# Thirty-two bytes more between the buffers of three tile pools in a one-core decoder trunk

## The chip, the core and the metric

The kernel runs on one core of one Trainium2 chip. The metric is the time of one execution in microseconds (us), the median of a few runs. TensorE multiplies, VectorE (DVE in the profile) and ScalarE (ACT) do the elementwise work, GpSimd (POOL) a little of it, and SyncE (SP) issues the loads of the weights. A matrix product is two instructions: a load of the stationary operand (LDWEIGHTS, the row PEld of the profile) and the streaming of the moving operand (MATMUL, the row PE). Both operands come from the on-chip memory SBUF, which has 128 partitions. A tile lies at the same byte address in every partition. In this document the **place** of a tile is its byte address in the partition modulo 128.

## The reference

Two decoder layers on 256 tokens of width 1024, all in float32. Cut to what matters:

```python
def swiglu_ffn(x, w_in, w_out):                # w_in 1024 x 5632, w_out 2816 x 1024
    gate, up = jnp.split(x @ w_in, 2, axis=-1)
    return (jax.nn.silu(gate) * up) @ w_out

for i in range(2):
    if i == 1:
        kv = shared_kv(h, ...)                 # K and V of three branches, once
    h = h + 0.5 * swiglu_ffn(rmsnorm(h, ffn1_norm[i]), ffn1_w_in[i], ffn1_w_out[i])
    hn = rmsnorm(h, mix_norm[i])
    if i == 0:
        h = h + short_conv_mixer(hn, ...)      # gated 3-tap convolution, two projections
    else:
        h = h + nsa_mixer(hn, ..., kv)         # sparse attention, 16 heads of 64
    h = h + 0.5 * swiglu_ffn(rmsnorm(h, ffn2_norm[i]), ffn2_w_in[i], ffn2_w_out[i])
```

## The kernel before

Tokens stand in the free dimension. Each number is split in two parts, a rounded high part and the rest, both of type float32r. A product of two numbers is then high x high, low x high and high x low. `ScalarE` casts the high part and `VectorE` subtracts to get the low part, for the weights as they arrive (`Stream.high` L250 and `Stream.low` L278, into the tiles `wh` and `wl`) and for the activations.

The normed activations are eight tiles of the pool `xs` (`new_xs`, L395), one for each 128 of the 1024 channels, with 512 columns: 256 tokens high and 256 tokens low. `a_pass` (through `half`, L487) takes a 128x128 piece of `wh` as the stationary operand and streams all 512 columns of one `xs` tile past it, then a piece of `wl` with the 256 high columns alone. So a projection is a long row of alternating groups: matmuls of 512 columns with `wh`, matmuls of 256 columns with `wl`. `xs` tiles are also the stationary operand in the query projection (`q_step`, L1398 to L1400), and hold copied probabilities in attention.

The second projections of three of the feed-forwards go through a blocked product that saves multiplications (`Blocks.product`, L821). There the activations are stationary and the weights stream, always 512 columns. Its stationary tiles are mostly `act`; the sums that it needs of activations lie in the pools `pr` and `hm` (`first_home` L793, `sum_home` L1665), and a few of its streamed weight sums in `pr`, `t2` and `xs` (`second_home`, L318). In attention `pr` holds the scores and probabilities of a head (`minima` L1480, `exps` L1492), and `hm` the values `V` (L1099).

The order of all work is written out by hand or follows from the code; tiles take the next free buffer of their pool. A pool gives each tag as many buffers as asked for, side by side, each as large as the largest tile of that tag. SBUF is filled in this order: constants, among them `ones` at byte 640 (place 0) and `base` at byte 1152; a 32-byte tile; then `ws`, `xs` (from byte 53792), `sq`, `kt`, `wh`, `wl`, `t2`, `t1`, `R`, `act`, `pr`, `sm`, `hm`, `u`, `rc`. All of the large buffers from `ws` to `hm` measure a multiple of 128 bytes (`xs` 2048, `wh` 4096, `act` 2048, `pr` 3072, `hm` 2048), and 24 `sm` buffers of 64 bytes make up 1536. So every large buffer has place 32. Pieces inside them begin at multiples of 512 bytes, so nearly every matmul of type float32r has both operands at place 32. Tiles that differ: `ones` has place 0, the identity in `small` place 0, the residual stream and the staged weights inside `base` place 80, and `vc` place 64.

Of the kernel before, what the change touches and what calls it, by code (L numbers as in the profile page):

```python
# [10 lines left out]
F32R = mybir.dt.float32r  # L11
# [5 lines left out]
P = 128  # L17
# [45 lines left out]
def trunk(ctx, tc, A, out):  # L63
# [11 lines left out]
    def mk(shape, tag, bufs, dt=F32, pool=None):  # L75
        uid[0] += 1
        return (pool or sb).tile(list(shape), dt, tag=tag, name=f"{tag}_{uid[0]}", bufs=bufs)
# [10 lines left out]
    def act(shape=(P, 512), dt=F32R):  # L88
        return mk(shape, "act", 22, dt)
# [4 lines left out]
    def t1(shape=(P, T)):  # L94
        return mk(shape, "t1", 6)

    def sm(shape):
        return mk(shape, "sm", 24)
# [294 lines left out]


    def new_xs():  # L395
        return [mk([P, 512], "xs", 8, F32R) for _ in range(8)]

    class Norm:

# [299 lines left out]


    xs = new_xs()
    nm = Norm([(xs, G_FFN1)])

# [92 lines left out]
    X = {}  # L796
# [161 lines left out]
    def conv_norm():  # L958
        X["xs"] = new_xs()
        X["nm"] = Norm([(X["xs"], G_MIX)])  # L960
        return X["nm"]
# [29 lines left out]
    xs, nm = X["xs"], X["nm"]  # L991
    for f in range(1, 8):
# [18 lines left out]
        weave(todo, 1 if f == 7 else 3)  # L1011

    xs = new_xs()
    nm = Norm([(xs, G_FFN2)])
    tab = tables()
# [80 lines left out]


    KC = (16, 272)
    V = [mk([P, 512], "hm", 5) for _ in range(2)]  # L1099

    vc = one([P, 2, 2, 64], "vc", F32R)
    zero = t2()
# [49 lines left out]
    xs = new_xs()  # L1152
# [3 lines left out]
    for tt in range(2):  # L1156
        ac.activation(V[tt], ov[tt], AF.Copy, scale=rc[:, tt:tt + 1])
    W.limit = 5
# [161 lines left out]
    xs = new_xs()  # L1320
# [158 lines left out]

    def minima(j, g2):  # L1480
        s, t = X.pop(("s", j, g2)), bias[j][:, g2, ::-1]
        X["pr", j, g2], X["mx", j, g2] = pr, mx = mk([P, 768], "pr", 6), sm([P, 16])
        for n, (a, b) in enumerate(SC):
            c0, w = REG[n]
            ve.tensor_tensor_reduce(out=pr[:, c0:c0 + w], in0=t[:, 128:256] if n < 2 else t, in1=s[:, a:b], op0=ALU.add, op1=ALU.min,  # L1485
                                    scale=1.0, scalar=3e38, accum_out=mx[:, n:n + 1])
        if ("cb", j // 2) not in X:
            X["cb", j // 2] = t1([P, 2, 2, 2, 16])
        ve.tensor_tensor(out=X["cb", j // 2][:, j % 2, :, g2], in0=cbias[:, j, :, g2],
                         in1=s[:, :576].rearrange("p (a b) -> p a b", a=2)[:, :, :16], op=ALU.add)  # L1490
# [40 lines left out]
    def copied(key, t, eng):  # L1531
        eng(out=t, in_=X.pop(key))
        X["p", *key[1:]] = t

    def value_codes(j, first=False):
        if first:
            X["v", j] = bank([P, T])
        pe.matmul(X["v", j], vc[:, j // 4].rearrange("p g d -> p (g d)"), ct.pop(j), start=first, stop=not first)

    def values(j, part=""):  # L1540
# [3 lines left out]
        for b in range(2):  # L1544
            for g2 in range(2):
                rows, c0 = slice(g2 * 64, g2 * 64 + 64), b * 256 + (2 * pp + g2) * 64
                pe.matmul(o[rows], V[0][:, c0:c0 + 64], lo[g2][:, b], start=(b == 0 and part != "n"), stop=False)  # L1547
        for b in range(2):
            for g2 in range(2):
                rows, c0 = slice(g2 * 64, g2 * 64 + 64), b * 256 + (2 * pp + g2) * 64  # L1550
                pe.matmul(o[rows, P:], V[1][:, c0:c0 + 64], hi[:, g2, b], start=False, stop=(b == 1 and part == "n"))
        X["v", j] = o
# [59 lines left out]
    def wo_part(c, part):  # L1612
# [10 lines left out]
        "SQ": q_square, "RD": q_reduce, "PW": q_power, "NW": q_newton, "QM": q_normed, "QT": q_trans, "QC": q_gain,  # L1623
        "F": lambda: next(lq), "GT": g_sum, "GC": g_copy, "GA": g_total, "GX": g_trans, "GE": g_exp, "GD": g_out,
        "S": scores, "M": minima, "E": exps, "R": recip,
        "N": lambda j, g, e="": normed(j, g, ve if e else po), "T": trans, "H": trans_hi,
        "C": lambda j, g, e="": copied(("t", j, g), mk([P, 2, T], "xs", 8), copy[e]),
        "CH": lambda j, e="": copied(("t", j), act([P, 2, 2, P], F32), copy[e]),
        "V": values, "VB": lambda j: value_codes(j, True), "O": out_hi, "P": out_lo,
        "CM": c_min, "CX": c_less, "CE": c_exp, "CR": c_recip, "CG": c_gate, "CI": c_high, "CL": c_low, "CP": c_trans,  # L1630
# [10 lines left out]
    xs = new_xs()  # L1641
# [189 lines left out]
```

## Time and profile before

| what | value |
|---|---|
| median of 3 runs | 959.15 us (958.61 to 959.93) |
| the profiled execution, its own time | 959.4 us |
| span of the profiled execution, first to last instruction | 957.5 us |
| granted TensorE clock, mean | 1.000 |
| VectorE busy | 803.5 us (84%) |
| ScalarE busy | 613.0 us (64%) |
| GpSimd busy | 144.5 us (15%) |
| DMA, mean over the span | 187 GB/s |

Busy time is the sum over an engine's instructions, with overlaps counted once. TensorE's matmuls overlap one another, since a matmul's record reaches until its last column has left the array. The mean duration of a matmul row is therefore longer than the distance from one start to the next. What a matmul costs in a long row of matmuls is that distance, called the **pitch** here.

### The profile page before, as it was taken

The numbers are of one execution on the slowest core, as the hardware profiler recorded it, in microseconds if no ns is written. First come the engines' busy times: TensorE is split into PE (matmuls) and PEld (weight loads), VectorE is DVE, ScalarE is ACT, GpSimd is POOL, SyncE is SP. The second block draws the span as 40 slices with busy tenths as digits, with TensorE's granted clock in tenths as the row PEclk, the third lists the DMA queues.
The fourth block names the chain that finished last, engine by engine and source line by source line (L and its number), as shares of the span: only waits on it lengthen the run. The fifth ranks groups of instructions, "written<-read, shape, count | busy, mean of one in ns | idle before, by whom it ended". The sixth has DMA issues, their size and how long they took to land.

```text
span 957.5 us, 14525 instructions
## 1 busy us (share of the span) xinstructions
PE 951.2 (99%) x5431; PEld 827.5 (86%) x5431; DVE 803.5 (84%) x1332; ACT 613.0 (64%) x1048; POOL 144.5 (15%) x231
## 2 busy tenths in 40 slices
PE   8999999999999999999999999999999999999998
PEld 7888888888888888888888898889987888888887
DVE  6898899898898888898969787866588888878996
ACT  7666565565556666565857777754579656656553
POOL 1000000024460000000021042001337350000002
PEclk9999999999999999999999999999999999999999
DMA  8665844364546567553636867554520363467452
GB/s 300 230 216 186 307 149 160 132 208 164 201 138 243 197 208 254 175 196 132 220 132 188 265 212 259 177 201 163 215 89 2 132 221 143 166 222 247 148 179 84
DMA packets 42150, 178.58 MB, mean 187 GB/s; under 512 B 3777, under 2 KB 7505, under 8 KB 27105
## 3 DMA queue, kind: packets, MB, share of 16 engines
q1 hardware_dynamic: 42080, 177.67, 54.1%
q8 instruction: 42, 0.69, 0.3%
q14 instruction: 28, 0.22, 0.1%
HBM read 175.52 MB, written 1.08 MB: 184 GB/s over the span
## 4 chain that ended last, share of the span: by engine, by line
PE 97%; DVE 1%; ACT 1%; DMA 1%; SPq 0%; issue 0%
PE mm L487 55%; PE a L487 13%; PE a L821 12%; PE mm L821 5%; PE a L1124 1%; PE mm L1477 1%; PE a L1547 1%; PE mm L728 1%; PE a L1522 1%; PE a L767 1%; DMA base<-in_first_dram 1%; DVE pr L1485 0%; PE a L1217 0%; PE a L1063 0%; PE a L1065 0%; PE a L1064 0%
## 5 line engine op out<-in xcount | busy, mean ns | idle before, releaser
L487 PE MATMUL mm<-xs,wh 128*128 128x512 f32 x1480 | 349.2, 390 | 0.0
L487 PEld LDWEIGHTS mm<-xs,wh 128*128 128x128 f32 x1480 | 273.6, 188 | 54.8 <-DVE xs L410 0.5
L278 DVE TENSOR_TENSOR wl<-ws,wh 128x1024 fp32r<-128x1024 f32 x217 | 271.1, 1258 | 28.2 <-ACT wh L250 18.4
L250 ACT CAST wh<-ws 128x1024 fp32r<-128x1024 f32 x217 | 224.6, 1045 | 14.9 <-PE a L487 7.3
L487 PEld LDWEIGHTS mm<-xs,wl 128*128 128x128 f32 x1480 | 185.2, 192 | 4.2
L487 PE MATMUL mm<-xs,wl 128*128 128x256 f32 x1480 | 187.3, 283 | 0.0
L506 DVE TENSOR_TENSOR t<-mm,t 128x512 f32<-128x512 f32 x95 | 65.2, 686 | 46.2 <-ACT t L505 45.5
L505 ACT COPY t<-mm 128x512 f32<-128x512 f32 x95 | 55.4, 583 | 52.5 <-PE mm L487 51.8
L821 PE MATMUL a<-wh,act 128*128 128x512 f32 x306 | 81.7, 390 | 0.0
L821 PEld LDWEIGHTS a<-wh,act 128*128 128x128 f32 x306 | 57.3, 188 | 11.8
L530 ACT ACTIVATE t<-t 128x256 f32<-128x256 f32 x88 | 36.8, 418 | 45.9 <-DVE t L517 45.7
L487 PE MATMUL a<-act,wh 128*128 128x512 f32 x256 | 60.0, 390 | 0.0
L487 PEld LDWEIGHTS a<-act,wh 128*128 128x128 f32 x256 | 47.5, 188 | 9.4
L499 ACT CAST act<-t 128x256 fp32r<-128x256 f32 x81 | 33.0, 407 | 29.1 <-DVE t L944 18.5
L406 ACT ACTIVATE xs<-base 128x256 fp32r<-128x256 f32 x32 | 16.1, 508 | 50.1 <-DVE base L637 35.2
L517 DVE TENSOR_TENSOR t<-t,R 128x256 f32<-128x256 f32 (+1 forms) x88 | 45.0, 511 | 2.6
L821 PE MATMUL a<-wl,act 128*128 128x512 f32 x153 | 46.9, 389 | 0.0
L184 DVE TENSOR_TENSOR wl<-base,wh 128x1024 fp32r<-128x1024 f32 x38 | 45.6, 1221 | 0.1
L531 DVE TENSOR_TENSOR t<-t,t 128x256 f32<-128x256 f32 x88 | 37.0, 420 | 4.1 <-ACT t L530 4.1
L500 DVE TENSOR_TENSOR act<-t,act 128x256 fp32r<-128x256 f32 x81 | 35.5, 438 | 4.7 <-ACT act L499 4.7
L173 ACT CAST wh<-base 128x1024 fp32r<-128x1024 f32 x33 | 33.6, 1045 | 4.8 <-DVE base L179 3.0
L821 PEld LDWEIGHTS a<-wl,act 128*128 128x128 f32 x153 | 28.7, 188 | 6.0
(361 smaller groups left out, 1405.5 us busy)
## 6 DMA issues: line engine op xcount, KB each, us to landing
ws<-in_ffn_w_in_dram SPq DMA_DIRECT2D x69, 1024.0 KB, 4.9
base<-in_ffn_w_pairs_dram SPq DMA_DIRECT2D x32, 512.0 KB, 4.8
ws<-in_conv_w_in_dram SPq DMA_DIRECT2D x12, 1024.0 KB, 4.8
ws<-in_ffn_w_pairs_dram SPq DMA_DIRECT2D x22, 512.0 KB, 4.9
ws<-in_ffn_w_out_dram SPq DMA_DIRECT2D x11, 1024.0 KB, 4.8
base<-in_ffn_w_in_dram SPq DMA_DIRECT2D x11, 1024.0 KB, 5.3
kt<-in_ffn_w_pairs_dram SPq DMA_DIRECT2D x12, 512.0 KB, 4.5
ws<-in_w_kv_dram SPq DMA_DIRECT2D x6, 1024.0 KB, 4.9
```

The source lines that it names most:

```text
L173: ac.copy(h, src)
L184: ve.tensor_tensor(out=l, in0=src, in1=h.bitcast(F32), op=ALU.subtract)
L250: ac.copy(h, src)
L278: ve.tensor_tensor(out=l, in0=src, in1=h.bitcast(F32), op=ALU.subtract)
L487: pe.matmul(o if x == 0 else o[:, :T], u[x][:, q * P:(q + 1) * P], rhs if x == 0 else rhs[:, :T], start=start, stop=stop, skip_group_check ...
L500: ve.tensor_tensor(out=dst[:, T:], in0=src, in1=dst[:, :T].bitcast(F32), op=ALU.subtract)
L505: ac.copy(r, o[:, :, T:])
L506: ve.tensor_tensor(out=r, in0=o[:, :, :T], in1=r, op=ALU.add)
L517: ve.tensor_tensor(out=r, in0=r, in1=R[:, None, :].to_broadcast([P, n, T]), op=ALU.mult)
L530: ac.activation(s, r[:, 0], AF.Silu)
L531: ve.tensor_tensor(out=s, in0=s, in1=r[:, 1], op=ALU.mult)
L821: pe.matmul(self.m[n], x, w, start=(c == 0), stop=(c == 3 * self.total[n] - 1), skip_group_check=True)
```

## The change

Three pools ask for buffers that are 8 floats, or 32 bytes, longer; the tiles themselves are cut back to their old size.

```diff
     def new_xs():
-        return [mk([P, 512], "xs", 8, F32R) for _ in range(8)]
+        return [mk([P, 520], "xs", 8, F32R)[:, :512] for _ in range(8)]
...
-    V = [mk([P, 512], "hm", 5) for _ in range(2)]
+    V = [mk([P, 520], "hm", 5)[:, :512] for _ in range(2)]
...
     def minima(j, g2):
         s, t = X.pop(("s", j, g2)), bias[j][:, g2, ::-1]
-        X["pr", j, g2], X["mx", j, g2] = pr, mx = mk([P, 768], "pr", 6), sm([P, 16])
+        X["pr", j, g2], X["mx", j, g2] = pr, mx = mk([P, 776], "pr", 6)[:, :768], sm([P, 16])
```

Since all buffers of a tag are as large as its largest tile, this moves every tile of the three pools, also those that other lines ask for. The places of the buffers, in the built program:

| pool | places before | places after |
|---|---|---|
| `xs`, 8 buffers | all 32 | 32, 64, 96, 0, 32, 64, 96, 0 |
| `pr`, 6 buffers | all 32 | 32, 64, 96, 0, 32, 64 |
| `hm`, 5 buffers | all 32 | 96, 0, 32, 64, 96 |
| `sm`, 24 small buffers | 32 and 96 in turn | 96 and 32 in turn |
| `u`, 2 buffers | 32, 64 | 0, 32 |
| `rc`, 2 buffers | 96 | 64 |
| `ws`, `kt`, `wh`, `wl`, `t2`, `t1`, `R`, `act` | 32 | 32 |

The eight longer `xs` buffers add 256 bytes, so what lies between `xs` and `pr` is moved by 256 bytes and keeps its place. The instructions of all engines, their order and their waits are the same in both programs. Only addresses differ. Of the 4,975 float32r matmuls, 16 had operands at different places before the change. After it there are 2,692: 1,332 with 512 columns and 1,360 with 256.

## The prediction

> **What bounds the kernel now.** I read the page's busy times first, then the chain that ended last, then TensorE's waits.
>
> ```profile
> PE 951.2 (99%) x5431; PEld 827.5 (86%) x5431; DVE 803.5 (84%) x1332; ACT 613.0 (64%) x1048; POOL 144.5 (15%) x231
> PE 97%; DVE 1%; ACT 1%; DMA 1%; SPq 0%; issue 0%
> ```
>
> TensorE is busy for 951.2 of 957.5 us, and the chain is TensorE for 97% of its length. Its waits, all of them:
>
> ```profile
> PE mm L728 <- ACT wh L719: 1.4, 2, 1.1
> PE a L376 <- DVE ones L356: 1.1, 1, 1.1
> PE a L1528 <- DVE xs L1532: 0.3, 1, 0.3
> PE a L1522 <- ACT xs L1532: 0.2, 1, 0.2
> ```
>
> They add up to 3.0 us (us in total, times, longest). So the time is the number of matmuls times the pitch of each, plus little. A change of addresses can act in two ways: through the pitch, or through the durations of the other engines where TensorE waits for them.
>
> The pitch comes from the timeline, from one start to the next. For 512 columns I take a stretch of the blocked product; its first and last rows:
>
> ```profile
> 905.80 0.62 PE L821 MATMUL mm<-wl,pr 128*128 128x512 f32 x2
> ...
> 923.25 0.61 PE L821 MATMUL a<-wh,act 128*128 128x512 f32 x2
> ```
>
> The rows from the first up to the last count 77 matmuls, and 923.25 - 905.80 = 17.45 us, so the pitch is 226.6 ns. For 256 columns a stretch of the convolution layer serves:
>
> ```profile
> 199.75 0.28 PE L487 MATMUL mm<-xs,wl 128*128 128x256 f32 x1
> 199.87 0.40 PE L465 MATMUL a<-t,ones 128*128 128x256 f32 x2
> 200.11 1.12 PE L487 MATMUL mm<-xs,wl 128*128 128x256 f32 x8
> 201.07 1.12 PE L487 MATMUL a<-xs,wl 128*128 128x256 f32 x8
> 202.03 1.32 PE L487 MATMUL mm<-xs,wh 128*128 128x512 f32 x5
> ```
>
> Between 200.11 and 202.03 there are 16 matmuls of 256 columns: 1.92 / 16 = 120.0 ns. The 256 columns more of the long one cost 226.6 - 120.0 = 106.6 ns. A matmul therefore costs its columns and about **13.4 ns more** (120.0 - 106.6), whatever its length. That surplus is what a change of places could touch. All float32r operands here, but for 16 matmuls, lie at place 32, so moving and stationary operand always share a place. After the change 2,692 float32r matmuls have unlike places, 2,676 more than before.
>
> **The change part by part: the matmuls.** The edit of `xs` gives most of these 2,676; the edits of `pr` and `hm` give those of the blocked product with a sum as an operand. Is the surplus a collision of two streams at one place? The trace has a small test of it. The stretch above holds two matmuls of the norm's row sums, `a<-t,ones`: `t` has place 32, the stationary `ones` place 0. The load of the second `ones` is the row
>
> ```profile
> 199.88 0.19 PEld L465 LDWEIGHTS a<-t,ones 128*128 128x128 f32 x1
> ```
>
> and the first of the two matmuls streams `t` from 199.87 on, so the load falls into a stream at another place. The two take 200.11 - 199.87 = 0.24 us, 120 ns each, the same as the 256-column neighbours whose places agree. Without the surplus they would take 2 x 106.6 = 213 ns, which would show as 0.21. So the surplus was paid where the places differ. This is one pair, and its only unlike case is 0 against 32.
>
> The second view asks whether any other traffic in SBUF slows a stream. Two input projections with the same code, half a millisecond apart, are these pieces of the chain:
>
> ```profile
> 289.10 111.85 PE mm L487 x644
> 785.72 111.85 PE mm L487 x644
> 289.10:400.95 111.85, 111.85 (x646) 99.03 (x645) 94.96 (x156) 69.85 (x109) 2.65 (x7) 1.00 0.64 220
> 785.72:897.57 111.85, 111.85 (x646) 99.03 (x645) 94.95 (x159) 69.71 (x109) 0.00 (x0) 1.00 0.52 179
> ```
>
> (The lower rows show the window, its length, busy time and count of PE, PEld, DVE, ACT and POOL, the granted clock, the DMA share and GB/s.) With DMA at 64% or 52%, and GpSimd at 2.65 us or none, the 644 matmuls take the same 111.85 us. Half of them have 512 columns and half 256, and 322 x (226.6 + 120.0) = 111.6 us; the pitch alone fills the section. The stream does not notice what others read or write, so moving their targets should not matter to it.
>
> I take **0** for the matmuls. Both ends are kept: if the surplus goes for all 2,676, the gain is 2,676 x 13.4 ns = 35.9 us; if unlike places cost as much again, the loss is 35.9 us. The nearest row is the `ones` pair, and it says 0.
>
> [...]
>
> **The change part by part: the other engines.** VectorE and ScalarE write or read the moved tiles. Operands at two places are already in the trace: tiles in `base` have place 80, `ws` and `kt` place 32.
>
> ```profile
> L184 DVE TENSOR_TENSOR wl<-base,wh 128x1024 fp32r<-128x1024 f32 x38 | 45.6, 1221 | 0.1
> L184 DVE TENSOR_TENSOR wl<-ws,wh 128x1024 fp32r<-128x1024 f32 x27 | 32.3, 1221 | 0.0
> L173 ACT CAST wh<-base 128x1024 fp32r<-128x1024 f32 x33 | 33.6, 1045 | 4.8 <-DVE base L179 3.0 <-DMA base<-in_ffn_w_pairs_dram 1.8
> L173 ACT CAST wh<-ws 128x1024 fp32r<-128x1024 f32 x22 | 22.5, 1048 | 0.9 <-DVE ws L179 0.9
> ```
>
> On VectorE the mean is 1221 ns from either place beside `wh` at 32; on ScalarE it is 1045 and 1048 ns. The largest difference is 3 in 1045, or 0.3%. What is on the path of these engines' work on moved tiles is small. In attention, the longest such piece of the chain and the row of its group are
>
> ```profile
> 713.47 3.52 ACT pr L1496 x16
> L1496 ACT ACTIVATE pr<-pr,sm 128x256 f32<-128x256 f32 x32 | 16.0, 508 | 0.0
> ```
>
> 0.3% of 3.52 us is 0.01 us. The two waits for `xs` at L1522 and L1528 sum to 0.5 us; if they went the gain is 0.5 us, and if they doubled the loss is 0.5 us. I take 0, nearest to the equal durations, and keep +-0.5 us. The rest of these engines' work on moved tiles stands beside the matmuls: VectorE is busy 94.96 of 111.85 us in the fullest section, so it could grow by 16.89 us there, 17.8% of its own work, before that section's matmuls had to wait on its mean rate. No DMA lands in the three pools, and no instruction or wait is added, removed or moved.
>
> **The sum.** Against the profiled execution: 959.4 + 0 (matmuls) + 0 (other engines, +-0.5) = 959.4 us. That is its span of 957.5 us and 1.9 us around it. The median of the runs shown, 959.15, lies 0.25 us lower; I predict the median after as 959.2 us.
>
> **The rivals.**
>
> Faster: the surplus is a collision of two streams at one place, and unlike places remove it. Then 959.4 - 35.9 = 923.5 us, if the splitting of weights keeps up, and VectorE's 94.96 of 111.85 us leaves the room. For it: nearly all pairs are at one place now, and every pitch has the surplus. Against it: the `ones` pair pays the surplus with unlike places. A part of it, say for one of the three new offsets, gives a third, 947.4 us, which the pair at its one offset does not exclude. Chance 0.11.
>
> Slower: a collision that does not exist now is made. Two streams that start at one place might keep step, and with unlike places the load would meet the moving stream on the same part of the memory somewhere in its course. As much again as the surplus would give 959.4 + 35.9 = 995.3 us; a third, 971.4 us. It decides from 1.9 / 2,676 = 0.7 ns a matmul on, since 0.2% of the time, 1.9 us, is about what a measurement of this kernel can tell from no change. For it: no row shows a stream of the length of the projections at unlike places. Against it: the same `ones` pair, at 120 ns, is not slower than its neighbours. Chance 0.09.
>
> That the change doesn't do what it says is not among them: the built addresses show the four places.
>
> **How the numbers follow.** The forecast has 0.80 for itself: the pair at unlike places, the two equal sections, and equal durations from places 32 and 80 all say that places don't matter, and nothing else changes. Faster has 0.11, slower 0.09. The range must hold 0.8. The forecast's own spread is what runs differ by (958.61 to 959.93), with 0.5 us for the waits and some room for a partial effect of about 1 ns a matmul either way, 2.7 us. I take 956.5 to 962.0 us, which leaves out most of both rivals.
>
> **What would show it right or wrong.** Right: the two sections stay at 111.85 us for 644 matmuls, the pitch at 226.6 and 120.0 ns, and L410, L1485 and L1496 keep their means. Wrong through the pitch: the sections get shorter or longer by the same share. Each has three quarters of its 644 matmuls at unlike places, 483, so a full surplus gained or lost would be 6.5 us, and a third 2.2 us. Wrong through the engines: the pitch stays, and TensorE's waits at L1522 and L1528 change. Were the rivals' effects both present at different offsets, the sections' mean would hide them, and the pitch of each `xs` tile would have to be read alone.

## The result and the profile after

| | median us | runs | lowest to highest |
|---|---|---|---|
| before | 959.12 | 4 | 958.61 to 959.93 |
| after | 963.95 | 4 | 963.75 to 964.11 |

The ratio is 1.0052 (95%: 1.0039 to 1.0064). The change makes the kernel about 4.8 us slower. That lies outside the predicted range, 956.5 to 962.0.

The page after the change, and then TensorE's waits (us in total, times, longest); they answer to the rows at the head of the prediction (the chain's shares are the same as there):

```profile
PE 956.4 (99%) x5431; PEld 824.8 (86%) x5431; DVE 804.9 (84%) x1332; ACT 613.6 (64%) x1048; POOL 144.5 (15%) x231
```

```profile
PE a L376 <- DVE ones L356: 1.0, 1, 1.0
PE mm L728 <- ACT wh L719: 0.6, 2, 0.4
PE a L1528 <- DVE xs L1532: 0.4, 1, 0.4
PE a L1522 <- ACT xs L1532: 0.2, 1, 0.2
```

TensorE's busy time grew by 5.2 us (951.2 to 956.4), the span by 4.6 us (957.5 to 962.1). The waits sum to 2.2 us, 0.8 us less than before. So nobody keeps TensorE waiting: its own matmuls take longer. The long pieces in the chain of waits say in which stages (start, length, count):

```profile
24.55 106.32 PE mm L487 x608
290.31 112.64 PE mm L487 x644
495.46 78.34 PE mm L487 x448
788.92 112.77 PE mm L487 x644
```

Before, the first and third of these were 105.59 and 77.82 us, and the two of 644 matmuls 111.85. Every stage grew, by 0.5 to 0.9 us. The timeline shows which of the two kinds of matmul did it. TensorE in the last of these stages, before and then after (start, length, count):

```profile
789.91 4.00 PE L487 MATMUL mm<-xs,wl 128*128 128x256 f32 x32
793.74 7.44 PE L487 MATMUL mm<-xs,wh 128*128 128x512 f32 x32
801.02 4.00 PE L487 MATMUL mm<-xs,wl 128*128 128x256 f32 x32
```

```profile
793.19 3.93 PE L487 MATMUL mm<-xs,wl 128*128 128x256 f32 x32
796.96 7.60 PE L487 MATMUL mm<-xs,wh 128*128 128x512 f32 x32
804.39 3.93 PE L487 MATMUL mm<-xs,wl 128*128 128x256 f32 x32
```

Take differences of starts. 32 matmuls of 256 columns took 3.83 us and take 3.77: the pitch falls from 119.7 to 117.8 ns. 32 of 512 columns took 7.28 us and take 7.43: it rises from 227.5 to 232.2 ns. **Two effects of opposite sign** share each stage, and its length shows only their difference.

The same on the whole trace, from the start of each matmul to the next, summed over a group and compared with before (the stretches in which TensorE waits are in the sums):

| group | matmuls | mean pitch before, after (ns) | change (us) |
|---|---|---|---|
| 512 columns, `xs` past `wh` (L487) | 1,536 | 228.3, 232.5 | +6.55 |
| 256 columns, `xs` past `wl` (L487) | 1,536 | 119.9, 117.8 | -3.10 |
| blocked product (L821), all its pairs | 735 | | +1.53 |
| everything else | | | -0.4 |
| sum | | | +4.57 |

In the blocked product it is the tiles of the moved pools that lengthen. The view of line L821, before and then after (shortest/median/longest record in ns):

```profile
L821 PE MATMUL mm<-wh,act x67: 389/389/389, 131.7 to 941.2; 128*128 128x512 f32 x67
L821 PE MATMUL mm<-wh,pr x48: 389/389/389, 137.9 to 916.7; 128*128 128x512 f32 x48
L821 PE MATMUL mm<-wh,hm x39: 389/389/389, 163.0 to 940.9; 128*128 128x512 f32 x39
```

```profile
L821 PE MATMUL mm<-wh,act x67: 388/389/398, 132.1 to 945.7; 128*128 128x512 f32 x67
L821 PE MATMUL mm<-wh,pr x48: 389/393/404, 138.3 to 921.0; 128*128 128x512 f32 x48
L821 PE MATMUL mm<-wh,hm x39: 387/394/398, 163.7 to 945.4; 128*128 128x512 f32 x39
```

`act`, which kept its place, keeps its median of 389; `pr` and `hm` go to 393 and 394. Before the change all records of these groups were equal to the nanosecond, and now they scatter. The ends of matmul records are modelled, so the records only point at the tiles; the sums in the table go by starts.

VectorE and ScalarE hardly changed: they are busy for 804.9 and 613.6 us, 1.4 and 0.6 us more than before. The groups of operations on moved tiles and on `wl` after the change:

```profile
L184 DVE TENSOR_TENSOR wl<-base,wh 128x1024 fp32r<-128x1024 f32 x38 | 45.6, 1221 | 0.1
L1496 ACT ACTIVATE pr<-pr,sm 128x256 f32<-128x256 f32 x32 | 16.0, 510 | 0.0
```

The first is the same as before, the second 2 ns longer, 0.4%, or 0.06 us over its 32 runs. The other two groups that the prediction named, L410 and L1485, keep their means of 576 and 417 ns.

### The profile page after: what moved, and what is told of

It is laid out like the page before. It is cut to its first block, busy times and chain, and to the rows that moved or that the text cites. A ratio compares the mean times of both kernels' runs of the same rounds, so it can differ in the third digit from the quotient of the medians.

```text
span 962.1 us, 14525 instructions
## 1 busy us (share of the span) xinstructions
PE 956.4 (99%) x5431; PEld 824.8 (86%) x5431; DVE 804.9 (84%) x1332; ACT 613.6 (64%) x1048; POOL 144.5 (15%) x231
## 4 chain that ended last, share of the span: by engine, by line
PE 97%; DVE 1%; ACT 1%; DMA 1%; SPq 0%; issue 0%
PE mm L487 55%; PE a L487 13%; PE a L821 12%; PE mm L821 6%; PE a L1124 1%; PE mm L1477 1%; PE a L1547 1%; PE a L1522 1%; PE mm L728 1%; PE a L767 1%; DMA base<-in_first_dram 1%; DVE pr L1485 0%; PE a L1217 0%; PE a L1063 0%; PE a L1065 0%; PE a L1064 0%
## 5 line engine op out<-in xcount | busy, mean ns | idle before, releaser
L487 PE MATMUL mm<-xs,wh 128*128 128x512 f32 x1480 | 355.4, 395 | 0.0
L487 PEld LDWEIGHTS mm<-xs,wh 128*128 128x128 f32 x1480 | 273.5, 188 | 60.2 <-DVE xs L442 0.2
L487 PEld LDWEIGHTS mm<-xs,wl 128*128 128x128 f32 x1480 | 182.4, 189 | 4.8
L487 PE MATMUL mm<-xs,wl 128*128 128x256 f32 x1480 | 184.5, 281 | 0.0
L505 ACT COPY t<-mm 128x512 f32<-128x512 f32 x95 | 55.4, 583 | 57.4 <-PE mm L487 56.8
L821 PE MATMUL a<-wh,act 128*128 128x512 f32 x306 | 82.1, 391 | 0.0
L821 PEld LDWEIGHTS a<-wh,act 128*128 128x128 f32 x306 | 57.3, 188 | 12.3
L487 PE MATMUL a<-act,wh 128*128 128x512 f32 x256 | 60.1, 390 | 0.0
L487 PEld LDWEIGHTS a<-act,wh 128*128 128x128 f32 x256 | 47.5, 188 | 9.5
L821 PE MATMUL a<-wl,act 128*128 128x512 f32 x153 | 47.0, 390 | 0.0
L184 DVE TENSOR_TENSOR wl<-base,wh 128x1024 fp32r<-128x1024 f32 x38 | 45.6, 1221 | 0.1
L821 PEld LDWEIGHTS a<-wl,act 128*128 128x128 f32 x153 | 28.7, 188 | 6.1
```

Source lines behind the costliest of these rows:

```text
L184: ve.tensor_tensor(out=l, in0=src, in1=h.bitcast(F32), op=ALU.subtract)
L487: pe.matmul(o if x == 0 else o[:, :T], u[x][:, q * P:(q + 1) * P], rhs if x == 0 else rhs[:, :T], start=start, stop=stop, skip_group_check ...
L505: ac.copy(r, o[:, :, T:])
L821: pe.matmul(self.m[n], x, w, start=(c == 0), stop=(c == 3 * self.total[n] - 1), skip_group_check=True)
```

## The experiments

The theory after the result: what counts is where a matmul's moving operand lies against the stationary one that is being loaded or used. Rivals: that it is the step from one place to the next between matmuls (before, no tile changed place), or that some other engine's or DMA's access to the moved tiles meets the stream. Eleven runs follow, the last of them the changed kernel again. "Distance" below is the address of the moving operand minus that of the stationary one.

### Places alone: `micro_places`

It has rows of 32 equal matmuls, and nothing else of the program runs beside them. It ran once. The core of it:

```diff
+        for i in range(count):
+            m = ((places[i % len(places)] - base) % 128 + places[i % len(places)] // 128 * 128) // 4
+            w = ((s - base) % 128) // 4 + i % 8 * 128
+            pe.matmul(b[:, :cols], st[:, w:w + 128], mv[:, m:m + cols], start=(i == 0), stop=(i == count - 1))
```

> This kernel computes none of the reference: after two fills it only runs groups of 32 float32r matmuls, with nothing beside them, at chosen places (byte address modulo 128) of the moving and the stationary operand, with 512 and with 256 columns; in some groups the place of the moving operand goes round from one matmul to the next. Theory A (the place of the moving operand against that of the stationary one sets the pitch): the groups with like places have 226.7 and 120 ns, those with unlike constant places about 231 to 233 and 117 to 118 ns, and the group that goes round 0, 32, 64, 96 lies between, about three quarters of the way. Theory B (the change of place from one moving operand to the next sets it): every group with a constant place has 226.7 and 120 ns, and only the groups that go round have about 232 and 118 ns. Theory C (the traffic of the other engines to the moved tiles makes the loss): all groups have 226.7 and 120 ns.

The timeline of its TensorE, for 512 columns and the stationary operand at place 32; the moving one is at place 0, 32, 64 and 96 in the first four rows, and the fifth begins the next set:

```profile
52.56 7.62 PE L70 MATMUL odd<-mv,st 128*128 128x512 f32 x32
60.02 7.42 PE L70 MATMUL even<-mv,st 128*128 128x512 f32 x32
67.28 7.63 PE L70 MATMUL odd<-mv,st 128*128 128x512 f32 x32
74.75 7.50 PE L70 MATMUL even<-mv,st 128*128 128x512 f32 x32
82.09 7.62 PE L70 MATMUL odd<-mv,st 128*128 128x512 f32 x32
```

From start to start: 7.46, 7.26, 7.47 and 7.34 us, or 233.1, 226.9, 233.4 and 229.4 ns. Only place 32, the like one, has the pitch of the kernel before. The same for 256 columns:

```profile
193.63 3.94 PE L70 MATMUL even<-mv,st 128*128 128x256 f32 x32
197.41 4.00 PE L70 MATMUL odd<-mv,st 128*128 128x256 f32 x32
201.25 3.94 PE L70 MATMUL even<-mv,st 128*128 128x256 f32 x32
205.02 3.93 PE L70 MATMUL odd<-mv,st 128*128 128x256 f32 x32
208.79 3.80 PE L70 MATMUL even<-mv,st 128*128 128x256 f32 x32
```

118.1, 120.0, 117.8 and 117.8 ns: here the like place is the **slowest**. All 16 combinations of four places agree in the 512-column rows: like places give 226.9 to 227.5 ns whichever the place is, unlike ones 229.1 to 234.4. Going round the four places from one matmul to the next gives 231.6 to 231.9 ns, within 1.2 ns of the mean of the four single rows, 230.7. So neither the place itself nor the change between matmuls is the cause, and no other engine is at work. One row didn't fit: the moving operand alternating between places 32 and 160 past a stationary one at 32 took 230.3 ns, though 160 and 32 are the same place modulo 128.

### One part of the change at a time: `xs_only` and `sums_only`

`xs_only` has only the edit of `new_xs`, `sums_only` only those of `hm` and `pr`.

> Only the xs buffers are 32 bytes longer; pr and hm as before. If the loss sits in the projections (theories A and B): nearly all of it is here, 963.0 to 964.0 us, and the two sections of 644 matmuls take 112.6 to 112.8 us as in the changed kernel. If the sum pools carry it: 959 to 960 us and sections of 111.85 us.

> Only the pr and hm buffers are 32 bytes longer; xs as before. Theories A and B: 959 to 960 us; the sections of 644 matmuls stay at 111.85 us, and the blocked product loses at most 0.5 us in all. If the sum pools carry the loss: 963 to 964 us.

| run | median us (runs) | ratio to before, 958.82 (13 runs) | its groups on the trace |
|---|---|---|---|
| `xs_only` | 962.54 (4) | 1.0038 (1.0024 to 1.0053) | 512 columns past `wh` +6.58 us, 256 columns past `wl` -3.13 us |
| `sums_only` | 960.15 (10) | 1.0013 (1.0004 to 1.0023) | blocked product +1.43 us, both `xs` groups unchanged |

The two parts add up: 3.7 + 1.3 = 5.0 us, beside the 4.8 us that the whole change costs. `xs_only` came out 0.5 us under its expected 963 to 964 us, with its sections at 112.64 and 112.77 us as expected. `sums_only` missed: its expectation allowed the blocked product 0.5 us, and it lost 1.43. In `sums_only`, the chain's last section of 644 matmuls, and then from the view of L821 the pair of `wh` and `pr`:

```profile
785.94 111.85 PE mm L487 x644
```

```profile
L821 PE MATMUL mm<-wh,pr x48: 388/394/404, 137.1 to 917.1; 128*128 128x512 f32 x48
```

The projections keep 111.85 us to the hundredth while the blocked product takes its loss alone. Each stage pays for its own operands.

### One constant distance: `xs_shifted`

All `xs` buffers are moved by 32 bytes, so no matmul differs from its neighbour in place; every `xs` tile is unlike the weights.

```diff
+    mk([P, 8], "pa", 1)
     xs = new_xs()
+    mk([P, 24], "pb", 1)
```

> All eight xs buffers are moved by 32 bytes to place 64 and keep their old distance of 2048 bytes; everything else keeps place 32. So moving and stationary operands of the projections have unlike places throughout, but the moving place does not change from one matmul to the next. Theory A: about a third more matmuls are unlike than in the changed kernel, sections of 112.6 to 113.0 us and 964 to 965 us. Theory B: sections of 111.85 us and 959 us, as before the change. Theory C (writes of the other engines to unlike places): near 959 us, since all writes go to one place.

Measured: 966.41 us, ratio 1.0078 (1.0061 to 1.0095). TensorE's timeline, and then the chain's last section of 644:

```profile
794.97 3.96 PE L487 MATMUL mm<-xs,wl 128*128 128x256 f32 x32
798.76 7.66 PE L487 MATMUL mm<-xs,wh 128*128 128x512 f32 x32
806.26 3.96 PE L487 MATMUL mm<-xs,wl 128*128 128x256 f32 x32
```

```profile
790.68 113.63 PE mm L487 x644
```

Without any change of place between matmuls the loss is larger than that of the change: the 512-column pitch is (806.26 - 798.76) / 32 = 234.4 ns, the 256-column one 118.4 ns. Over the trace that is +9.48 and -2.45 us. Theory A has the direction, but its expectation was too low by 1.4 us and by 0.6 us a section. The rival of the step between places falls. The buffers behind `xs`, `wh` and `wl` among them, moved by 128 bytes in this kernel, so its distance is 32 - 128 = -96 bytes, which matters for the next run.

### Which period: `micro_scan` and `xs_plus256`

`micro_scan` is `micro_places` with one operand fixed and the other moved in steps, in rows of 40. It too ran once.

```diff
+            m, w = i % 8 * 512 + d // 4, i % 8 * 128
+            pe.matmul(b[:, :cols], st[:, w:w + 128], mv[:, m:m + cols], start=(i == 0), stop=(i == count - 1))
```

> This kernel computes none of the reference: groups of 40 float32r matmuls with nothing beside them. The stationary pieces begin at one and the same byte modulo 512; the moving pieces, eight tiles 2048 bytes apart, begin a constant number of bytes past it, from 0 to 496, the same for a whole group. Theory A1 (the place modulo 128 alone counts): distances of 0, 128, 256 and 384 bytes all have 226.7 and 120 ns, distances of 32, 64 and 96 bytes about 233, 229 and 233 ns with 512 columns and 118 ns with 256. Theory A2 (the two operands' distance counts over more than 128 bytes): only the distance 0 has 226.7 and 120 ns; 128 and 256 bytes differ from it. Where some distance gives less than 120 ns with 256 columns in all groups near it, that is what a better layout would use.

Its TensorE timeline for 512 columns; the rows are the distances 0 and 16, then 128 and 144, then 256 and 288:

```profile
25.80 9.23 PE L58 MATMUL odd<-mv,st 128*128 128x512 f32 x40
34.87 9.43 PE L58 MATMUL even<-mv,st 128*128 128x512 f32 x40
44.13 9.50 PE L58 MATMUL odd<-mv,st 128*128 128x512 f32 x40
...
99.79 9.46 PE L58 MATMUL odd<-mv,st 128*128 128x512 f32 x40
109.09 9.48 PE L58 MATMUL even<-mv,st 128*128 128x512 f32 x40
...
137.07 9.23 PE L58 MATMUL odd<-mv,st 128*128 128x512 f32 x40
146.14 9.50 PE L58 MATMUL even<-mv,st 128*128 128x512 f32 x40
```

Distance 0 takes 9.07 us (226.7 ns), 16 takes 9.26 (231.5), 128 takes 9.30 (232.5), and 256 again 9.07. In full, from starts, in ns:

| distance, bytes | 0 | 16 | 32 | 48 | 64 | 80 | 96 | 112 | 128 | 144 | 192 | 224 | 256 | 320 | 416 |
|---|---|---|---|---|---|---|---|---|---|---|---|---|---|---|---|
| 512 columns | 226.7 | 231.5 | 233.5 | 233.2 | 229.0 | 231.2 | 233.5 | 231.0 | 232.5 | 233.0 | 233.2 | 233.2 | 226.7 | 229.0 | 234.0 |
| 256 columns | 120.0 | 118.8 | 116.7 | 118.3 | 117.7 | 119.5 | 120.0 | 113.8 | 118.5 | 118.8 | 114.0 | 118.3 | 119.7 | 117.7 | 117.5 |

**The pattern repeats after 256 bytes, not after 128.** Neither theory holds as it was put: 128 bytes are not like 0 (A1), and 256 bytes are (against A2). That explains the odd row of `micro_places` (the mean of the entries at 0 and 128 is 229.6 ns; measured 230.3), and it says what the change does: with buffers 2,080 bytes apart, the eight `xs` tiles stand at all eight multiples of 32 modulo 256, so only one in eight is like the weights, not two. By the built addresses of the changed kernel 1,558 matmuls of 512 columns and 1,584 of 256 have unlike operands by this measure (before: 4 and 16). The mean of the scan over the eight distances (taking 416 for 160) is 232.0 and 117.8 ns; the kernel has 232.5 and 117.8. `xs_shifted`, at -96 or 160 modulo 256, fits as well: 234.4 and 118.4 ns beside 234.0 and 117.5 at 416.

The mean holds, though not each tile: in the changed kernel the `xs` tile at distance 0 has a mean of 233.4 ns past `wh` (median 230), where the scan has 226.7 in a steady row, and the one at distance 32 has 229.4, where the scan has 233.5. In the kernel the neighbours stand at other distances, so something carries over from one matmul to the next.

`xs_plus256` moves `xs` by 256 bytes (two helper buffers of 64 floats instead of the 8 and 24 above).

> All eight xs buffers are moved by 256 bytes, so that their place modulo 128 stays 32 like that of all others; the rest keeps its address modulo 512. In the changed kernel, too, the weights lie 256 bytes further against the first xs buffer. Theory A1 (place modulo 128 alone): nothing changes, 958.8 us and sections of 111.85 us. Theory A2 (distance over more than 128 bytes): the sections change, and the time moves by more than 1 us either way, by the amounts of the group at a distance of 256 bytes in the scan.

Measured: 958.85 us beside 958.95, ratio 0.9999 (0.9989 to 1.0008). Its chain:

```profile
288.27 111.85 PE mm L487 x644
784.89 111.85 PE mm L487 x644
```

`xs` and all that lies behind it have moved, and nothing changes, as the scan's equal rows at 0 and 256 say. That a tile moves costs nothing; what counts is its distance modulo 256.

### Keeping the gain without the loss: `wl_shifted`, `wl_plus64`, `wl_plus144`

If like places are best at 512 columns and worst at 256, then `wh` should stay and `wl` should move, since only 256-column matmuls stream past `wl` in the projections. Three kernels did that with helper buffers before and behind `wl`:

```diff
-        w = [[mk([P, 2, 4, P], t, NBUF, F32R) for t in ("wh", "wl")] for _ in range(4)]
+        w = [[mk([P, 2, 4, P], "wh", NBUF, F32R)]]
+        mk([P, 8], "pa", 1)
+        w[0].append(mk([P, 2, 4, P], "wl", NBUF, F32R))
+        mk([P, 120], "pb", 1)
+        w += [[mk([P, 2, 4, P], t, NBUF, F32R) for t in ("wh", "wl")] for _ in range(3)]
```

This is `wl_shifted`, 32 bytes. `wl_plus64` has 16 and 112 floats, `wl_plus144` 36 and 92.

> Only the wl buffers (low parts of the weights) are moved, by 32 bytes to place 64; xs, wh, act and the rest keep their address modulo 512. So matmuls with wh keep like places, and those with wl get unlike ones. Theory A, from the groups measured alone: about 1,850 matmuls of 256 columns at 117.8 in place of 120.0 ns are 4.1 us less; about 230 matmuls of 512 columns of the blocked product with wl streaming at 233.2 in place of 226.7 ns are 1.5 us more; in all about 956.2 us, faster than the kernel before by 2.6 us, with the sections of 644 matmuls at 111.1 us. If unlike places only ever cost (the slower rival as it stood in the prediction): slower than 958.8 us, with sections above 111.85 us.

> Only the wl buffers are moved, by 64 bytes; the rest keeps its address modulo 512. The matmuls of xs with wl get a distance of 192 bytes (moving less stationary, modulo 256), for which the scan measured 113.35 ns with 256 columns in place of 120.0; those of the blocked product with wl streaming get 64 bytes, 229.0 in place of 226.7 ns. Theory A2 with the scan's numbers: about 1,824 x 6.65 ns = 12.1 us less, 230 x 2.3 ns = 0.5 us more, and, from the kernel with wl moved by 32 bytes, some 2 to 3 us more at the changes between wh and wl; 948 to 950 us, sections of 644 matmuls at about 110 us. If the fast spacing of 113.35 ns needs a longer undisturbed row than the kernel's groups of 8 to 32 matmuls, the pitch is 117.7 ns and the time 958 to 960 us.

> Only the wl buffers are moved, by 144 bytes; the rest keeps its address modulo 512. The matmuls of xs with wl get a distance of 112 bytes, the other one with 113.35 ns in the scan; those of the blocked product with wl streaming get 144 bytes, 233.4 ns. Theory A2 with the scan's numbers: 12.1 us less, 230 x 6.7 ns = 1.5 us more, and 2 to 4 us more at the changes between wh and wl: 949 to 952 us, sections at about 110 us. If the distance modulo 128 alone counted, 112 bytes would be like 16 bytes before the stationary operand, about 118 ns, and the time near 961 us.

| run | median us (runs) | before us (runs) | ratio |
|---|---|---|---|
| `wl_shifted` | 961.48 (9) | 958.95 (19) | 1.0026 (1.0016 to 1.0035) |
| `wl_plus64` | 958.13 (11) | 958.87 (15) | 0.9991 (0.9982 to 1.0000) |
| `wl_plus144` | 964.75 (5) | 958.87 (15) | 1.0061 (1.0048 to 1.0074) |

`wl_shifted` was expected to gain and lost; the expectation missed. The sections did shrink (111.69 us, below), but the blocked product grew by 3.03 us, since there `wl` is the moving operand, with 512 columns, past a stationary `act` that hadn't moved. Of the 3.03 us, the matmuls with `wl` streaming have 1.45 and those of `wh` past `act`, whose own operands are alike, 1.20. The chain's last section of 644, and then from the groups the pair of `wl` and `act` in the blocked product (mean 389 ns before), now at L825:

```profile
786.77 111.69 PE mm L487 x644
```

```profile
L825 PE MATMUL a<-wl,act 128*128 128x512 f32 x153 | 47.8, 395 | 0.0
```

The trace holds one more hint. In the projections the last matmul of `xs` past `wh` before each change to `wl` went from a mean of 226.9 to 234.7 ns (52 such places at L487), although its own two operands are still alike; what is unlike is the stationary piece loaded next, while it streams. So there it seems to be the load of the next stationary operand that meets the stream, not the one already in the array. It isn't so at every distance: in `wl_plus64`, where the stream begins 192 bytes past the piece loaded next (modulo 256) and not 224, the same 52 matmuls take 226.3 ns.

`wl_plus64` reached 111.19 us in both sections of 644, but its 256-column pitch was 117.8 ns on the timeline, where the scan has 114.0 at that distance (192), so it won less than expected (the expectation's 113.35 ns is under the scan's two best rows as well, 113.8 and 114.0). The blocked product took 2.4 us back, where 0.5 was expected: its matmuls with `wl` streaming, at a distance of 64, have a mean of 234.4 ns, and the scan has 229.0 there. Both misses say that a row of the scan can't be carried over one by one to a kernel in which `wh` and `wl` take turns. It ends 0.7 us below before, at the limit of what can be told.

`wl_plus144` didn't do what its expectation describes. In the built program buffers begin at multiples of 32 bytes, so `wl` moved by 160 bytes and not by 144, and all that lies behind it by 544, which is 32 modulo 256. That made `act` unlike `wh`. On the trace the output projections (`act` past `wh`, L487) cost 1.55 us more and `wh` past `act` in the blocked product 2.15 us more. The row of the first, whose mean was 390 ns before:

```profile
L487 PE MATMUL a<-act,wh 128*128 128x512 f32 x256 | 61.5, 395 | 0.0
```

It says nothing of a distance of 144, but it tests the scan at other operands, and there most rows fit: `act` past `wh`, now 32 bytes apart, has a mean of 233.6 ns (scan 233.5); `wh` past `act` in the blocked product, at 224, 233.0 (scan 233.2); and `xs` past `wl`, at 96, stays at 119.9 (scan 120.0). `wl` past `act`, at 128, has 231.1 (scan 232.5).

### A version that beats both: `wl_inside`, beside `after_again`

The buffers of `wl` grow to 1,056 floats, and the low weights of a projection lie 64 bytes into the buffer, so they are unlike the activations. Those of the blocked product start where their distance to `act` is a multiple of 256 bytes. Buffers of 4,224 bytes stand 128 apart modulo 256, so the start depends on which buffer is next, and a table holds that order.

```diff
+    def low_tile(at=None):
+        t = mk([P, 1056], "wl", NBUF, F32R)
+        odd = int(WL_SLOTS[wl_count[0]]) % 2
+        wl_count[0] += 1
+        at = 32 * odd if at is None else at
+        return t[:, at:at + 1024]
...
-                l = mk([P, 2, 512], "wl", NBUF, F32R)
+                l = low_tile().rearrange("p (a n) -> p a n", n=512)
...
-            l = mk([P, 1024], "wl", NBUF, F32R)
+            l = low_tile(16)
```

> The wl buffers are 128 bytes longer. Low weights for the plain projections stand 64 bytes into their buffer, so that xs and wl are 64 or 192 bytes apart (modulo 256); those for the blocked product stand 0 or 128 bytes into it, so that they keep a distance of 0 from the activations. All else keeps its address modulo 256. Theory A2, from the kernel with wl moved by 64 bytes: the sections stay at about 111.2 us, the 256-column matmuls at 118 ns, a gain of some 3 us, and the loss of 2.3 us in the blocked product is gone; 955 to 956.5 us, faster than the kernel before beyond noise. If the loss in the blocked product had another cause than the distance: 958 us.

> The changed kernel as it is, on the chip and in the call of the version above: 963.5 to 964.2 us by every theory; it serves as the comparison.

| run | median us (runs) | ratio to before, 959.06 (9 runs) |
|---|---|---|
| `wl_inside` | 954.26 (5) | 0.9950 (0.9937 to 0.9964) |
| the changed kernel again | 963.62 (4) | 1.0047 (1.0033 to 1.0061) |

The chain of `wl_inside`, and then its TensorE timeline (L505 is L487 of before):

```profile
288.38 110.19 PE mm L505 x644
781.53 110.75 PE mm L505 x644
```

```profile
785.71 3.91 PE L505 MATMUL mm<-xs,wl 128*128 128x256 f32 x32
789.46 7.44 PE L505 MATMUL mm<-xs,wh 128*128 128x512 f32 x32
796.74 3.93 PE L505 MATMUL mm<-xs,wl 128*128 128x256 f32 x32
```

512 columns stay at (796.74 - 789.46) / 32 = 227.5 ns and 256 columns fall to 117.2. Both sections and the time came out below the expectation (111.2 and 955 to 956.5 us). Over the trace, `xs` past `wl` gains 5.33 us, `act` past `wl` 0.85 us, and the blocked product keeps its means; the 512-column groups of both projections give 1.4 us back. The same address effect that made the change 4.8 us slower makes this version 4.8 us faster.

## Why the prediction was wrong

**What bounds the kernel: right.** TensorE's pitch sets the time before and after; its waits stayed at 2 to 3 us.

**The other engines, 0 +-0.5 us: right.** The means of L184 and L1496 moved by 0 and 2 ns, and the two waits for `xs` went from 0.5 to 0.6 us. Their traffic doesn't reach the matmuls either: `sums_only` moved targets of VectorE and ScalarE, and the projections stayed at 111.85 us; `xs_plus256` moved `xs` with the same outcome.

**The matmuls, "I take 0": this step failed.** In its place stand +6.55 us for `xs` past `wh`, -3.10 us for `xs` past `wl` and +1.53 us in the blocked product. The 0 rested on two rows that couldn't carry it.

The first was the `ones` pair, two matmuls of 256 columns with unlike places, 0.24 us. Three things are wrong with it as a test. It has 256 columns, and the sign of the effect turns over with the length: at 512 columns, the half of the projections that costs two thirds of the time, unlike places are slower. The prediction said itself that no row shows a stream of that length at unlike places, and gave that little weight. Then the timeline has steps of 0.01 us, 5 ns for each of two matmuls, and the effect at 256 columns is about 2 ns. A single pair couldn't have shown it on the timeline; read from the trace's starts in whole nanoseconds, the four such pairs of the kernel before take 235 to 237 ns, some 2 ns a matmul less than 120. And the pair gives one distance of eight (32 - 640 is 160 modulo 256, where the scan has 117.5 ns at 256 columns and 234.0 at 512).

The second was the two equal sections of 111.85 us under different traffic. That reading holds. But it says that the stream doesn't notice other engines, and the prediction drew from it that moving the operands should not matter. In both sections the operands stood at the same distance from each other, so the sections couldn't tell.

The trace of before also held a row of the missing length, hidden by counting modulo 128. The weights of the attention's gates (`g_sum`, L1436) are pieces of 96 columns, so they begin 384 bytes apart, and every second one lies 128 bytes off its `xs` tile modulo 256:

```profile
689.46 2.02 PE L1436 MATMUL a<-xs,wh 128*96 128x512 f32 x8
691.31 0.28 PE L1398 MATMUL a<-wh,xs 128*128 128x256 f32 x1
```

That is (691.31 - 689.46) / 8 = 231.2 ns, beside 226.6 in the blocked product. Its pieces are narrower than those of the projections, so it is a hint and no more, but it points to a loss.

**The surplus of 13.4 ns** was taken for a fixed price that is either a collision or not. It is the steady state of like places. Unlike places change it in both directions: from 226.7 to between 229.0 and 234.0 ns at 512 columns, and from 120.0 to between 113.8 and 120.0 at 256. At best, half of it goes.

**The rivals.** The slower one had the right sign and, as far as the runs show one, the mechanism: the next load meeting the moving stream when their places are unlike. `wl_shifted` speaks for it and `wl_plus64` against it at another distance, so it isn't shown as a whole. Its price was off. It set one size, 13.4 ns, and the third of it, 4.5 ns, for every unlike matmul, short and long. Measured in the kernel: 6.55 us / 1,536 = 4.3 ns more for the long ones with `xs`, 3.10 / 1,536 = 2.0 ns **less** for the short ones, 4.57 us in all, where the rival gave 12 us with a third of the surplus. The faster rival has the right sign for the 256-column matmuls alone, and there for 2.0 of its 13.4 ns. The prediction's last sentence saw that both could be present and that the sections' mean would hide them; it gave that case no chance of its own.

**The premise of the change.** By the scan its four places modulo 128 are eight modulo 256. The table of unlike matmuls ahead of the prediction, 2,692, counts by 128; by 256 it is 3,142.

Still open: what in the hardware has a period of 256 bytes; why a constant distance of 192 gives 114.0 ns in the scan and 117.8 in `wl_plus64`, and one of 64 with 512 columns 229.0 and 234.4; why an unlike next load slows a like matmul at 224 bytes and not at 192; and how the effect carries over from one matmul to the next. In the scan every row is steady, in the kernel groups at other distances stand between; no run separates what that does.

## What to carry to other kernels

In a stream of 512-column float32r matmuls that load new weights each time, keep the moving operand and the stationary operands a multiple of 256 bytes apart; pad other tiles so that this stays so, and check the built addresses of everything behind a padded pool. Where 256-column matmuls have stationary tiles of their own, those alone can be moved: here that gained 0.5% (`wl_inside`). Before an address or a size is called harmless, test it on the very shape that fills the time: an effect of 2 to 6 ns a matmul is under the step of a timeline row of two, and is plain in a row of 32. When a stage mixes two shapes, read the pitch of each, since the stage's length shows only the difference.

## What the runs showed of the hardware

- In steady rows a stream's pitch depends on where its operands lie against each other, modulo 256 bytes, with nothing else running: 226.7 to 234.0 ns for 512 columns, 113.8 to 120.0 ns for 256 (`micro_scan`). The Trainium skill, "TensorE: Matmul & The Clock Gate", section "Step-by-step: what each phase is for", says that loading the next weights doesn't take read bandwidth in SBUF from the running matmul, because the two have ports of their own. The scan changes only the two operands' distance and gets 3% at 512 columns, and in `wl_shifted` a matmul with like operands slowed by 7.8 ns when the piece loaded during it was unlike (in `wl_plus64`, at another distance, it didn't). For these float32r streams the measurement decides: the load and the stream are not independent of each other.
- The best distance for one length is the worst for the other: 0 is the fastest at 512 columns and shares the slowest value, 120.0 ns, with 96 at 256 columns.
- With like operands, traffic of GpSimd and of the DMAs left a section unchanged to 0.01 us in 111.85, and rows with nothing beside them have the same pitch, 226.7 and 120.0 ns (`micro_scan`). Unlike operands at one constant distance give two equal sections too, 113.63 us in `xs_shifted` and 111.19 us in `wl_plus64`, under the same two kinds of traffic. Only where the distance changes between tiles do the sections differ a little (112.64 and 112.77 us after the change, 110.19 and 110.75 in `wl_inside`); no run isolates why.
